# An encoder layer on one core: the first stage written in a new order, and silu(c) spread through a row in DRAM

## The chip, the cores and the metric

The kernel runs on one core of a Trainium2 chip. The core has five engines that run side by side, each through its own list of instructions, strictly in order: TensorE (PE in the profile, with its weight loads as PEld), VectorE (DVE), ScalarE (ACT), GpSimd (POOL) and SyncE (SP), which here issues the transfers (DMAs) between the device's memory and the on-chip memory. Engines wait for each other by semaphores. The metric is the device time of one execution in microseconds.

## The reference

One layer of an encoder over 2048 tokens of width 1024, batch 1, everything in float32. What matters for this change is how it begins:

```python
c_act = jax.nn.silu(c)                                   # c: 1024 numbers
mod = c_act @ ada_w[l] + ada_b[l]                        # 3 x 1024 numbers
shift, scale, gate = jnp.split(mod, 3, axis=-1)
h = (_layernorm(x) * (1.0 + scale[:, None, :]) + shift[:, None, :])
proj = h @ w_in[l]                                       # 1024 x 9216
...                                                      # recurrence and neighbourhood attention on proj's parts
y = jnp.concatenate([y_hg, y_na], axis=-1) @ w_out[l]
z = DEEPNORM_ALPHA * x + gate[:, None, :] * y
x = _layernorm(z) * ln_g[l] + ln_b[l]
```

## The kernel before

The first half of the tokens (1024) is held as two groups of 512 tokens, and the model's width as eight blocks of 128, called k = 0 to 7. A **piece** (g, k) is the part of h for group g and block k, turned so that the width lies on the partitions: 128 x 512 numbers, stored as a high and a low part (`h` tiles) because a product in float32 is made of three matmuls: high by high, low by high, high by low.

`startup` is the stage that the change touches. It makes all 16 pieces and multiplies each, as soon as it is there, with the weights of three projections (query, key and gate of the first attention pair), adding up over k in six PSUM tiles `acc`. Its parts, with the names and lines that the trace shows:

- **silu(c)**: `mod_init` loads c into all 128 partitions (`cb`, L133); `mod_silu` makes exp on ACT (L138), a cap on DVE (L318), Ln and Exp on ACT (L319, L320); the product is made in `startup` on DVE (L1197), between the second and the third tile of the norms.
- **modulation sums**: for each k, `mod_sum` (L150) makes two sums over 1024 products on DVE, one for `shift` and one for `scale`, from two 512 KB tiles `ada` of ada_w that `mod_load` (L145) fetches. Six such tiles fit, so a load waits for an earlier sum.
- **norms**: `x_stats` (L200, L201) takes mean and variance of the four tiles of 128 tokens of a group on DVE, `rstd_of` (L176 to L183) and L207 turn them into a factor and an offset by small steps on DVE and ACT, and `x_scale` (L214) applies them on ACT, to half of the width (four blocks) at a time.
- **a piece** (`h_piece`): four transposes on PE into PSUM (L221), scale and shift on ACT (L223, tile `sg`), the high part on ACT (L225), the low part on DVE (L228).
- **weights**: `w_load` (L1176) and `w_split`: high part on ACT (L1184), low part on DVE (L1185). They come in two halves, for k below 4 and from 4 on.
- **products**: `proj_mm` (L260), nine matmuls of 128x512 for each piece.

Within this stage the order of PE, SP, ACT and DVE is the order of the code. The list `order` says in which order the pieces are multiplied: group 0's first three, then group 1's first two, then alternating. `piece(g, k)` writes everything that the piece needs at the place of the piece: for group 0 its own modulation sum first, then transposes, scaling and split; for (1, 0) the whole norms of group 1 first. One piece ahead is written before the nine matmuls of the current one. So on PE the transposes of the next piece stand before the matmuls of the current piece.

After the stage, `first_half` begins: the six sums are copied out of PSUM (`evac`, L748), split into the tiles of the attention (q at L927 and L928, the copies `KA` and `KB` at L943, the gate at L958, L319, L320), while PE runs `vproj` (L273), a projection whose weights come in four tiles that are split at L800 and L801. The first two splits are made within `startup`, the third and fourth after the evacuations. In this part the order of PE is still that of the code; ACT, DVE and SP are ordered by a scheduler at build time. The results of vproj go out to DRAM (`nv`, L281) and come back in another layout (`V`, L952), which the attention's last product (L1074) reads. `gate_load` (L158, L161) fetches the rest of ada_w for the gate's sums, which use silu(c) from a DRAM row `c_d`.

Of the kernel before, what the change touches and what calls it, by code (L numbers as in the profile page):

```python
# [10 lines left out]
F32 = mybir.dt.float32  # L11
F32R = mybir.dt.float32r
U32 = mybir.dt.uint32
AF = mybir.ActivationFunctionType
ALU = mybir.AluOpType
# [22 lines left out]
def body(ctx: ExitStack, tc: tile.TileContext, t):  # L38
# [49 lines left out]
    def nm(s):  # L88
        cnt[0] += 1
        return f"{s}_{cnt[0]}"  # L90
# [40 lines left out]
    def mod_init():  # L131
        mod["c"] = tl("cb", shape=[P, D])
        dma(mod["c"], t["c"].rearrange("p k -> (p k)").rearrange("(o n) -> o n", o=1).to_broadcast([P, D]))  # L133

    def mod_silu():
        dve.tensor_scalar(adab1, adab[:, 8:16], 1.0, 1.0, op0=ALU.mult, op1=ALU.add)
        r = tl("nb", shape=[P, 3072])[:, 0:D]
        act.activation(r, mod["c"], AF.Exp, scale=-1.0)  # L138
        sigmoid(r)
        return r  # L140
# [54 lines left out]
    def x_stats(xs, pin=lambda x: x, between=None):  # L195
        mv = cp.tile([P, 4, 2], F32, tag="xmv", name=nm("xmv"), bufs=2)
        for i, xt in enumerate(xs):
            st = cp.tile([P, 2, 6], F32, tag="bnst", name=nm("bnst"), bufs=4)
            for a in range(2):
                pin(dve.bn_stats(st[:, a, :], xt[a]))  # L200
            dve.bn_aggr(mv[:, i, :], st)  # L201
            if i == 1 and between:
                between()
# [14 lines left out]
    def h_piece(xs, k, hi, lo, early=False):  # L218
# [5 lines left out]
        if early:  # L224
            act.activation(hi, tmp, AF.Copy)  # L225
        else:
            dve.tensor_copy(hi, tmp)
# [939 lines left out]
    def startup():  # L1167
# [25 lines left out]
        xs[1] = x_load(1)  # L1193
        for i in range(3):
            w_load(i, 1)
        r = mod_silu()
        how[0] = x_stats(xs[0], between=lambda: dve.tensor_mul(mod["c"], mod["c"], r))  # L1197
# [3 lines left out]
        order = [(0, 0), (0, 1), (0, 2), (1, 0), (1, 1), (0, 3), (1, 2), (0, 4), (1, 3), (0, 5), (1, 4), (0, 6), (1, 5), (0, 7), (1, 6), (1, 7)]  # L1201

        def piece(g, k):
            if g == 0:
                mod_sum(k)
                if k and k + 2 < KT:
                    mod_load(k + 2)
                if k == 0:
                    w_split(0, 0)
            elif k == 0:  # L1210
                how[1] = x_stats(xs[1])
                x_scale(xs[1], how[1], 0, 4)
            h_piece(xs[g], k, hts[g, k, 0], hts[g, k, 1], True)
            if (g, k) == (0, 0):
                w_split(1, 0)
                w_split(2, 0)
            elif (g, k) == (1, 1):
                x_scale(xs[0], how[0], 1, 4)
            elif (g, k) == (0, 3):
                for i in range(3):  # L1220
                    w_split(i, 1)
            elif (g, k) == (0, 4):
                x_scale(xs[1], how[1], 1, 4)

        piece(0, 0)
        for n, (g, k) in enumerate(order):
            if n + 1 < len(order):
                piece(*order[n + 1])
            if (g, k) == (0, 6):
                feed = Chunks(first_srcs())  # L1230
                rp = bias_rows()
                bias_fill()
                dma(lg, t["lb_logits"])
                dma(normg, t["hg_norm_g"])
            if (g, k) == (0, 7):
                bias_tables(rp)
                bias_pair(0)
                dma(c_d.rearrange("(o n) -> o n", o=1), mod["c"][0:1, :])
            if (g, k) in ((0, 7), (1, 6)):
                feed.split()  # L1240
            for i in range(3):
                proj_mm(acc[i, g], *ws[i], g, k)
            if (g, k) == (1, 7):
                for gg in range(2):
                    for i in range(3):
                        rows[NCOL[i][0]][gg] = evac(acc[i, gg])
# [353 lines left out]
```

## Time and profile before

| | us |
|---|---|
| three timed runs | 2669.26, 2673.63, 2672.89 |
| their median | 2672.89 |
| the execution that was profiled | 2663.61 |
| its span, from the first to the last instruction | 2661.8 |
| first matmul of the stage | 21.26 |
| first matmul of vproj, where the stage ends on PE | 89.45 |

The prediction quotes rows of views of one profiled execution. A row of a timeline has the start in us from the span's start, the duration, the engine, the line of the kernel, the operation, output<-input by the program's names, shapes and a count, and in brackets how long the engine sat idle before it and what released it. A row of waits has the engine and line that waited, what it waited for, the total, the number of times and the longest. A row of windows has the busy time of each engine in a stretch, the granted clock of TensorE and the share of the DMA engines. The chain is the work that ended last, followed backwards; within it "DMA a<-b" is the time until that transfer landed. "SPq" rows are SP issuing a transfer.

### The profile page before, as it was taken

What the parts mean: (1) busy time and instruction counts of PE and PEld (TensorE: products, weight loads), DVE (VectorE), ACT (ScalarE), POOL (GpSimd) and SP (SyncE); (2) the same over time, 40 slices, a digit from 0 to 9 for tenths busy, and PEclk for the clock granted to TensorE, in tenths of its full rate; (3) what the DMA queues carried; (4) which work ended last, traced back from release to release, by engine and by line L of the source; (5) the groups of instructions that cost most, each with busy time, mean ns of one, the idle gap of its engine ahead of it and who ended that gap; (6) DMA issues with size and microseconds to landing.
All of it is one profiled execution on the core that took longest, in us unless ns stands there. A gap on an engine that the chain in (4) does not pass through costs nothing.

```text
span 2661.8 us, 46149 instructions
## 1 busy us (share of the span) xinstructions
PE 2574.7 (97%) x17328; PEld 2151.1 (81%) x17328; DVE 1761.2 (66%) x4351; ACT 1417.6 (53%) x2808; POOL 105.3 (4%) x143
## 2 busy tenths in 40 slices
PE   4999999999999999999999999999999997999998
PEld 3888888888888888888888888887888886788887
DVE  5445445477777778877777877456877886548443
ACT  4434444376666667666666665355666665331110
POOL 0000000000000000000000000000000000032221
PEclk8999999999999999999999999999999998999999
DMA  6555454212222227312221122354444456554331
GB/s 232 169 176 161 144 179 139 99 64 100 84 80 80 88 96 252 105 58 76 72 80 60 65 72 79 101 165 114 124 135 139 130 144 168 143 158 131 95 95 56
DMA packets 235777, 313.25 MB, mean 118 GB/s; under 512 B 29480, under 2 KB 118312, under 8 KB 235433
## 3 DMA queue, kind: packets, MB, share of 16 engines
q1 hardware_dynamic: 235553, 310.30, 37.8%
q8 instruction: 136, 2.23, 0.4%
q14 instruction: 88, 0.72, 0.1%
HBM read 226.63 MB, written 75.37 MB: 113 GB/s over the span
## 4 chain that ended last, share of the span: by engine, by line
PE 87%; DVE 5%; DMA 4%; ACT 3%; issue 1%; SPq 0%; DVEq 0%; ACTq 0%
PE pj L260 49%; PE pj L273 5%; PE ps L1431 4%; PE ps L1430 4%; PE ps L1432 4%; PE ps L1074 3%; PE ps L1055 3%; PE ps L473 2%; PE ps L1006 2%; PE ps L465 1%; PE ps L1010 1%; PE ps L540 1%; PE ps L564 1%; PE ps L566 1%; PE ps L512 1%; DMA V<-nv 1%
## 5 line engine op out<-in xcount | busy, mean ns | idle before, releaser
L260 PE MATMUL pj<-h,wh 128*128 128x512 f32 x4016 | 1278.0, 399 | 10.6 <-ACT h L225 6.3
L260 PEld LDWEIGHTS pj<-h,wh 128*128 128x128 f32 x4016 | 730.9, 188 | 168.7 <-issue 13.1
L260 PE MATMUL pj<-h,wl 128*128 128x512 f32 x2008 | 785.8, 391 | 0.1
L260 PEld LDWEIGHTS pj<-h,wl 128*128 128x128 f32 x2008 | 377.2, 188 | 82.0 <-DVE wl L775 0.5
L1028 ACT ACTIVATE pbuf<-pbuf,mx 128x480 f32<-128x480 f32 (+2 forms) x224 | 143.1, 640 | 159.4 <-DVE mx L1023 158.5
L1023 DVE CUSTOM_DVE_ANT_1 pbuf<-ps,bias 128x480 f32<-128x480 f32 (+2 forms) x224 | 125.5, 589 | 117.5 <-PE ps L1010 95.7
L273 PE MATMUL pj<-wh,h 128*128 128x256 f32 x1024 | 193.6, 287 | 2.8 <-ACT vt L279 2.5
L273 PEld LDWEIGHTS pj<-wh,h 128*128 128x128 f32 x1024 | 162.7, 193 | 6.1 <-ACT vt L279 3.4
L251 DVE TENSOR_TENSOR wl<-wr,wh 128x512 fp32r<-128x512 f32 x192 | 131.5, 685 | 45.7 <-ACT wh L250 44.4
L250 ACT ACTIVATE wh<-wr 128x512 fp32r<-128x512 f32 x192 | 120.0, 625 | 73.2 <-PE pj L260 62.6
L273 PE MATMUL pj<-wl,h 128*128 128x256 f32 x512 | 145.5, 284 | 0.3 <-DVE wl L801 0.3
L1059 DVE COPY pt<-ps 128x512 f32<-128x512 f32 (+1 forms) x128 | 79.0, 618 | 58.9 <-PE ps L1055 58.1
L1061 ACT ACTIVATE pt<-ps 128x512 f32<-128x512 f32 (+1 forms) x128 | 68.9, 539 | 91.1 <-PE ps L1055 89.9
L459 DVE TENSOR_TENSOR de<-e,de 128x512 f32<-128x512 f32 x64 | 44.3, 692 | 109.2 <-ACT de L458 108.7
L748 ACT ACTIVATE e<-pj 128x512 f32<-128x512 f32 x100 | 59.1, 592 | 96.6 <-PE pj L260 85.7
L1055 PE MATMUL ps<-ident,pbuf 128*128 128x128 f32 x776 | 103.8, 274 | 1.5 <-DVE pt L1059 1.5
L1055 PEld LDWEIGHTS ps<-ident,pbuf 128*128 128x128 f32 x776 | 91.2, 141 | 15.5 <-DVE pt L1059 1.7
L1406 ACT ACTIVATE yh<-yr 128x512 fp32r<-128x512 f32 x52 | 32.7, 628 | 132.8 <-PE ps L1431 114.4
L1479 DVE TENSOR_TENSOR vt<-ps,gt 128x512 f32<-128x512 f32 x24 | 16.5, 691 | 127.1 <-PE ps L1432 127.1
L273 PEld LDWEIGHTS pj<-wl,h 128*128 128x128 f32 x512 | 98.8, 193 | 1.3 <-DVE wl L801 0.5
L1033 DVE TENSOR_SCALAR pbuf<-pbuf,mx 128x480 f32<-128x480 f32 (+2 forms) x224 | 95.7, 436 | 5.5
L801 DVE TENSOR_TENSOR wl<-wr,wh 128x512 fp32r<-128x512 f32 x68 | 46.8, 690 | 78.7 <-ACT wh L800 68.2
(273 smaller groups left out, 4757.3 us busy)
## 6 DMA issues: line engine op xcount, KB each, us to landing
wr<-in_w_in SPq DMA_DIRECT2D x276, 256.0 KB
V<-nv SPq DMA_DIRECT2D x256, 64.0 KB
yr<-yq SPq DMA_DIRECT2D x60, 256.0 KB
bias<-tint SPq DMA_DIRECT2D x24, 480.0 KB
x<-in_x SPq DMA_DIRECT2D x32, 256.0 KB
ada<-in_ada_w SPq DMA_DIRECT2D x16, 512.0 KB
wr<-in_w_v SPq DMA_DIRECT2D x32, 256.0 KB
nv<-vt SPq DMA_DIRECT2D x32, 256.0 KB
```

Of the source, the lines that this page charges most:

```text
L250: act.activation(hi, raw, AF.Copy)
L251: dve.tensor_tensor(lo, raw, hi, op=ALU.subtract)
L260: pe.matmul(pz, a, b, start=(k == 0 and n == 0), stop=(k == KT - 1 and n == 2))
L273: pe.matmul(pzs[tp][:, i * 256:(i + 1) * 256], a, b, start=(k == 0 and n == 0 and i == 0), stop=(k == KT - 1 and n == 2), skip_group_check ...
L1023: return dve.tensor_tensor_reduce(s[:, 0:nk].rearrange("p (r c) -> p r c", c=32), sc[:, 0:nk].rearrange("p (r c) -> p r c", c=32), bt[:, 0 ...
L1028: act.activation(s[:, 0:nk], s[:, 0:nk], AF.Exp, scale=-1.0, bias=mx[:, 0:1], accum_out=mx[:, 1:2])
L1033: dve.tensor_scalar(s[:, 0:nk], s[:, 0:nk], mx[:, 2:3], 1.0, op0=ALU.mult, op1=ALU.mult)
L1055: pe.transpose(ptp[:, c * P:(c + 1) * P], s[:, c * P:(c + 1) * P], ident)
L1074: pe.matmul(self.po[R][hs_, j * P:(j + 1) * P], self.st.V[c0 + c][:, j * P + hh * 64:j * P + hh * 64 + 64], pts[hh][:, c * P:(c + 1) * P], ...
L1430: pe.matmul(pz, yh[:, kk], wh, start=first, stop=False)
L1431: pe.matmul(pz, yh[:, kk], wl, start=False, stop=False)
L1432: pe.matmul(pz, yl[:, kk], wh, start=False, stop=last)
```

## The change

It rewrites the first stage. Nothing else of the program is edited; line numbers after it are a few higher.

- silu(c) is made on a 128 x 8 tile `cs` and not on 128 copies of c. The 4 KB result is written to the DRAM row `c_d` and read back from there into all partitions (`cb`). Both transfers are issued by ACT; no other transfer of the program is. The store of `c_d` that SP made at the end of the stage is gone.
- `x_stats` is split in `x_stat` (one tile) and `x_rate`, so that the norms of group 1 can be written tile by tile.
- `h_piece` gives its last step, the low part on DVE, back as a function, so that other work can be written between the high and the low part.
- Two tables, `ahead` and `after`, say what is written with which piece: the modulation sum of k stands with an earlier piece, the norms of group 1 with pieces (0, 2) and (0, 3), the splits of the second half of the weights with (1, 0), `x_scale` for the second half of the width with (1, 1).
- The order of the pieces has four of group 0 first.
- As a result of the scheduler's work, not of the text: in `first_half` SP now issues eight loads for the gate's sums (L161) ahead of the first loads V; before, all of them stood behind the first of those.
- On SP the loads of the sums of k = 3 come before the second group's x, and later loads are asked for one sum earlier.

```diff
     def mod_init():
         mod["c"] = tl("cb", shape=[P, D])
-        dma(mod["c"], t["c"]....to_broadcast([P, D]))
...
+        cs = [cp.tile([P, KT], F32, name=f"cs{i}") for i in range(2)]
+        dma(cs[0], t["c"])
+        act.activation(cs[1], cs[0], AF.Exp, scale=-1.0)
+        sigmoid(cs[1])
+        dve.tensor_mul(cs[1], cs[0], cs[1])
+        act.dma_start(c_d.rearrange("(p k) -> p k", k=KT), cs[1])
+        act.dma_start(mod["c"], c_d.rearrange("(o n) -> o n", o=1).to_broadcast([P, D]))
...
         if early:
             act.activation(hi, tmp, AF.Copy)
-        else:
-            dve.tensor_copy(hi, tmp)
+            return lambda: dve.tensor_tensor(lo, tmp, hi, op=ALU.subtract)
...
-        order = [(0, 0), (0, 1), (0, 2), (1, 0), (1, 1), (0, 3), (1, 2), (0, 4), (1, 3), ...
+        def mod_step(k):
+            mod_sum(k)
+            if k + 3 < KT:
+                mod_load(k + 3)
...
+        order = [(0, 0), (0, 1), (0, 2), (0, 3), (1, 0), (1, 1), (0, 4), (1, 2), (1, 3), ...
+        ahead = {(0, 0): [(mod_step, 1)], (0, 1): [(mod_step, 2)], (0, 2): [(mod_step, 3), (second_stats, 0)], (0, 3): [(second_stats, 1, 2, 3)],
...
         def piece(g, k):
-            if g == 0:
-                mod_sum(k)
...
+            low = head(g, k)
+            for f, *a in ahead.get((g, k), []):
+                f(*a)
+            low()
```

**ACT, at the start of the program.** `cb` is silu(c) or c in all partitions, `nb` a scratch tile, `cs` the small tile, L178 the first of ACT's two steps of group 0's norms. Before:

```order
L107 ACT_TABLE_LOAD
L138 ACTIVATE nb_194<-cb_136 128x1024
L319 ACTIVATE nb_194<-nb_194 128x1024
L320 ACTIVATE nb_194<-nb_194 128x1024
L178 ACTIVATE l_220<-v_218 128x4
```

And now:

```order
L107 ACT_TABLE_LOAD
L135 ACTIVATE cs_138<-cs_137 128x8
L323 ACTIVATE cs_138<-cs_138 128x8
L324 ACTIVATE cs_138<-cs_138 128x8
L138 DMA c_d<-cs_138 128x8
L139 DMA cb_136<-c_d 128x1024
L178 ACTIVATE l_204<-v_202 128x4
```

The three wide operations became three narrow ones, and two transfers stand ahead of L178; the second waits for the first to land.

**DVE, in the first pieces.** `h_96` and `h_98` are low parts of pieces (0, 1) and (0, 2); the pairs of L150 with two `ada` tiles are the sums of one k. Before, from the low part of (0, 1) on, where the sums belong to k = 2 and the statistics are those of group 1:

```order
L228 TENSOR_TENSOR h_96<-sg_273,h_95 128x512
L150 ISA ada_170,shift<-ada_170,cb_136,adab 128x1024
L150 ISA shift 128x1
L150 ISA ada_172,scale_86<-ada_172,cb_136,adab_84 128x1024
L150 ISA scale_86 128x1
L228 TENSOR_TENSOR h_98<-sg_297,h_97 128x512
L200 BN_STATS bnst_311<-x_174 128x6
L200 BN_STATS bnst_311<-x_175 128x6
```

And now, from the sums of k = 2 on, which are followed by those of k = 3:

```order
L150 ISA ada_180,shift<-ada_180,cb_136,adab 128x1024
L150 ISA shift 128x1
L150 ISA ada_182,scale_86<-ada_182,cb_136,adab_84 128x1024
L150 ISA scale_86 128x1
L230 TENSOR_TENSOR h_96<-sg_281,h_95 128x512
L150 ISA ada_226,shift<-ada_226,cb_136,adab 128x1024
L150 ISA shift 128x1
L150 ISA ada_228,scale_86<-ada_228,cb_136,adab_84 128x1024
L150 ISA scale_86 128x1
L204 BN_STATS bnst_314<-x_230 128x6
L204 BN_STATS bnst_314<-x_231 128x6
L205 BN_AGGR xmv_223<-bnst_314 128x2
```

The sums of a k stand one low part earlier, those of k = 3 were moved ahead of the statistics of group 1, and the low part `h_98` (not in these rows) now follows the first tile's statistics.

**ACT, at the end of the stage.** `e` are the six sums copied out of PSUM, `KA`, `KB` the key tiles, `sg` the gate, `wh` the third and fourth weight tile of vproj. Before:

```order
L748 ACTIVATE e_674<-ps_236 128x512
L958 ACTIVATE sg_724<-e_672 128x512
L748 ACTIVATE e_676<-ps_237 128x512
L748 ACTIVATE e_678<-ps_238 128x512
L319 ACTIVATE sg_724<-sg_724 128x512
L320 ACTIVATE sg_724<-sg_724 128x512
L800 ACTIVATE wh_731<-wr_558 128x512
L800 ACTIVATE wh_737<-wr_560 128x512
L943 ACTIVATE KA_163_697<-e_670 64x512
L943 ACTIVATE KB_164_698<-e_670 64x512
```

And now:

```order
L752 ACTIVATE e_676<-ps_220 128x512
L947 ACTIVATE KA_162_699<-e_672 64x512
L947 ACTIVATE KB_163_700<-e_672 64x512
L962 ACTIVATE sg_726<-e_674 128x512
L752 ACTIVATE e_678<-ps_221 128x512
L752 ACTIVATE e_680<-ps_222 128x512
L947 ACTIVATE KA_162_699<-e_678 64x256
L947 ACTIVATE KB_163_700<-e_678 64x256
L323 ACTIVATE sg_726<-sg_726 128x512
L324 ACTIVATE sg_726<-sg_726 128x512
L804 ACTIVATE wh_733<-wr_507 128x512
L804 ACTIVATE wh_739<-wr_509 128x512
```

The four key copies, which stood behind the two weight splits, now stand ahead of them; DVE's low parts moved in the same way.

More of the change, by code (lines that the diff above doesn't have):

```diff
@@ L193, in x_load, with x_stats, x_stat, x_rate @@
         return xs
-    def x_stats(xs, pin=lambda x: x, between=None):
+    def x_stats(xs, pin=lambda x: x):
         mv = cp.tile([P, 4, 2], F32, tag="xmv", name=nm("xmv"), bufs=2)
[L197 to L203, printed above, removed]
+        for i in range(4):
+            x_stat(xs[i], mv[:, i, :], pin)
+        return x_rate(mv)
+    def x_stat(xt, mv, pin=lambda x: x):
+        st = cp.tile([P, 2, 6], F32, tag="bnst", name=nm("bnst"), bufs=4)
+        for a in range(2):
+            pin(dve.bn_stats(st[:, a, :], xt[a]))
+        dve.bn_aggr(mv, st)
+    def x_rate(mv):
         r = cp.tile([P, 4], F32, tag="xr", name=nm("xr"), bufs=2)
@@ L1192, in startup @@
         mod_load(2)
[L1193 to L1197, printed above, removed]
+        how[0] = x_stats(xs[0])
         x_scale(xs[0], how[0], 0, 4)
@@ L1200, in startup @@
         rows = {n: [None, None] for n, _ in NCOL}
-        order = [(0, 0), (0, 1), (0, 2), (1, 0), (1, 1), (0, 3), (1, 2), (0, 4), (1, 3), (0, 5), (1, 4), (0, 6), (1, 5), (0, 7), (1, 6), (1, 7)]
-        def piece(g, k):
-            if g == 0:
-                mod_sum(k)
[L1206 to L1223, printed above, removed]
+        mv1 = cp.tile([P, 4, 2], F32, tag="xmv", name=nm("xmv"), bufs=2)
@@ new lines, in startup, with second_x, second_stats, head @@
+        more = {}
+        def mod_step(k):
+            mod_sum(k)
+            if k + 3 < KT:
+                mod_load(k + 3)
+        def second_x():
+            xs[1] = x_load(1)
+            for i in range(3):
+                w_load(i, 1)
+        def second_stats(*tiles):
+            for i in tiles:
+                x_stat(xs[1][i], mv1[:, i, :])
+            if 3 in tiles:
+                how[1] = x_rate(mv1)
+                x_scale(xs[1], how[1], 0, 4)
+        def head(g, k):
+            return h_piece(xs[g], k, hts[g, k, 0], hts[g, k, 1], True)
@@ L1225, in startup @@
+        def piece(g, k):
+            low = head(g, k)
+            for f, *a in ahead.get((g, k), []):
+                f(*a)
+            low()
+        mod_step(0)
+        second_x()
+        w_split(0, 0)
         piece(0, 0)
+        w_split(1, 0)
+        w_split(2, 0)
         for n, (g, k) in enumerate(order):
@@ L1228, in startup @@
                 piece(*order[n + 1])
[L1229 to L1240, printed above, removed]
+            for f, *a in after.get((g, k), []):
+                f(*a)
             for i in range(3):
                 proj_mm(acc[i, g], *ws[i], g, k)
[L1243 to L1246, printed above, removed]
+        for gg in range(2):
+            for i in range(3):
+                rows[NCOL[i][0]][gg] = evac(acc[i, gg])
+        feed = more["feed"]
         return rows, feed
```

23 lines of the change are left out of this document (17 added, 6 removed).

## Prediction

> **What bounds the kernel now.** The page first: PE is the bound of the whole.
>
> ```profile
> span 2661.8 us, 46149 instructions
> PE 2574.7 (97%) x17328; PEld 2151.1 (81%) x17328; DVE 1761.2 (66%) x4351; ACT 1417.6 (53%) x2808; POOL 105.3 (4%) x143
> ```
>
> PE lacks 87.1 us of the span. So the question is where PE idles, and I cut the first stage into windows at its breaks.
>
> ```profile
> core 0: us, PE busy (x) PEld busy (x) DVE busy (x) ACT busy (x) POOL busy (x), PEclk, DMA share, GB/s
> 0.00:17.20 17.20, 0.00 (x0) 0.00 (x0) 9.44 (x22) 5.79 (x8) 3.99 (x11) 1.00 0.89 316
> 17.20:29.90 12.70, 10.16 (x30) 6.43 (x30) 9.24 (x16) 6.38 (x10) 0.00 (x0) 1.00 1.04 396
> 29.90:43.20 13.30, 1.93 (x6) 0.98 (x6) 7.46 (x21) 4.74 (x8) 0.00 (x0) 0.59 0.40 161
> 43.20:89.40 46.20, 39.20 (x175) 29.25 (x174) 25.52 (x44) 28.15 (x44) 1.07 (x5) 0.97 0.39 116
> ```
>
> PE is idle 17.2, 2.5, 11.4 and 7.0 us, 38.1 of the 87.1. These are three different waits, and the view of waits up to 125 us and PE's timeline say which:
>
> ```profile
> PE ps L221 <- ACT x L214: 29.2, 8, 17.2
> ACT sg L223 <- DVE scale L150: 20.2, 7, 3.5
> PE pj L260 <- ACT h L225: 6.3, 7, 1.4
> ...
> 40.65 0.47 PE L221 MATMUL ps<-ident,x 128*128 128x128 f32 x1 [10.68 <-ACT x L214]
> 42.89 1.20 PE L260 MATMUL pj<-h,wh 128*128 128x512 f32 x2
> 46.48 0.60 PE L221 MATMUL ps<-ident,x 128*128 128x128 f32 x4
> 49.00 0.60 PE L221 MATMUL ps<-ident,x 128*128 128x128 f32 x4
> 89.45 0.28 PE L273 MATMUL pj<-wh,h 128*128 128x256 f32 x1
> ```
>
> The wait on L214 is for normalized tokens, once at the start (17.2) and once for group 1 (10.68). The second row is the repeated one: ACT waits 20.2 us for modulation sums, 2.9 each, and PE then for ACT. A piece that waits for nothing takes 49.00 - 46.48 = 2.52 us on PE. DVE's timeline shows why both waits are long:
>
> ```profile
> 7.11 0.69 DVE L318 TENSOR_SCALAR nb<-nb 128x1024 f32<-128x1024 f32 x1 [4.43 <-ACT nb L138]
> 7.72 1.28 DVE L200 BATCH_NORM_STATS2 bnst<-x 128x6 f32<-128x512 f32 x2
> 10.55 1.19 DVE L1197 TENSOR_TENSOR cb<-cb,nb 128x1024 f32<-128x1024 f32 x1
> 16.07 0.16 DVE L207 SCALAR_TENSOR_TENSOR xb<-xmv,xr 128x4 f32<-128x4 f32 x1
> 16.15 1.28 DVE L150 CUSTOM_DVE_ANT_0 ada<-ada,cb,adab 128x1024 f32<-128x1024 f32 x1
> 18.57 0.08 DVE L150 DVE_READ_ACCUMULATOR2_ANT scale<- 128x1 f32 x1
> 32.38 1.28 DVE L200 BATCH_NORM_STATS2 bnst<-x 128x6 f32<-128x512 f32 x2
> 39.58 0.16 DVE L207 SCALAR_TENSOR_TENSOR xb<-xmv,xr 128x4 f32<-128x4 f32 x1
> ```
>
> A pair of sums takes 2.42 us (16.15 to 18.57), two tiles of statistics 2.83 (7.72 to 10.55), all of group 1's norms 7.4 (32.38 to 39.74), during which nothing else is written. Afterwards DVE is busy only 25.5 of 46.2 us: each sum comes just too late, with free time between.
>
> **The change part by part.** First, silu(c). The chain's first rows:
>
> ```profile
> 1.20 4.80 DMA cb<-in_c
> 6.02 4.52 DMA x<-in_x
> ...
> 0.75 0.39 SPq L121 DMA_DIRECT2D adab<-in_ada_b  x1
> 2.52 0.17 DVE L136 TENSOR_SCALAR adab<-adab 128x8 f32<-128x8 f32 x1 [2.52 <-DMA adab<-in_ada_b]
> ...
> 96.16 0.47 SPq L1238 DMA_DIRECT2D c_d<-cb  x1
> 98.61 0.45 POOL L722 MEMSET bias<- 64x192 f32 x2 [12.46 <-DMA c_d<-cb]
> ```
>
> The load of c took 4.8 us, and x's last tile was issued only when it had landed (6.02): 512 KB that go. A small load landed 1.77 us after its issue, the 4 KB store 2.45. DVE loses the cap of 0.69 and the product of 1.19 in front of and inside the statistics. Without both, statistics begin with x's first tile, which I put at 4.4 (issue 1.7, latency 1.77 as adab, 0.65 for 256 KB at the 400 GB/s of the second window, rounded up); four tiles take 5.7, the small steps 1.7 (10.55 + 1.19 and two more tiles make 14.57, L207 ends at 16.23): ready at 11.8, say 12.0, in place of 16.2.
>
> On ACT: c lands at 3.0 (1.2 + 1.77), three narrow operations and two on DVE end at 4.3 (0.26 each, of which L207 shows 0.16 and the rest is handing over), the store lands at 6.8, and until then ACT stands still. Behind it is queued L178, which is due at 10.5, so the wait costs nothing, with 3.7 us to spare. The spread then takes 4.8 us as the load of c did: landed at 11.6, when the first sums are due at 12.0. This is the unknown: no transfer of this trace is issued by ACT. The nearest rows bound it from below at 9.9 (1.77 plus 1.3 for the bytes, behind nothing) and from above at 18, if it stands behind what SP has issued (worked out under the rivals). From 13 on (ACT's `x_scale` and the transposes, until 15.5, cover about 1 us) each us late costs one.
>
> [...]
>
> Then DVE is one chain up to group 1's norms, and I add it up: sums of k = 0 from 12.0 to 14.4; the first weight split waits for its high part on ACT behind four `x_scale` (2.93 below) until 15.5 and ends at 16.1; sums of k = 1 to 18.6; three 0.6 us subtractions to 20.4; sums of k = 2 to 22.8; one subtraction, sums of k = 3 to 25.9; a tile's statistics to 27.3; a subtraction, three tiles to 32.2; small steps to 34.0. So group 1's norms are ready at 34.0, not 39.7, with one k more of sums done. The loads keep up: up to those of k = 3 it is 7.6 MB, at 400 GB/s from 2.2 on until 21.2, and I allow 24.6 for latency and the spread; group 1's x lands by 30. The pieces (0, 0) to (0, 2) go by beside it.
>
> ```profile
> 39.78 2.93 ACT L214 ACTIVATE x<-x,xb,xr 128x512 f32<-128x512 f32 x4 [1.02 <-DVE xb L207]
> ```
>
> On PE the transposes of (1, 0) still stand ahead of the matmuls of the piece before it, now (0, 3). So these start 3.1 us after the norms, as before (39.78 to 42.89): at 37.1, a gain of 5.8. Behind that point before had 14 pieces and took 46.6 us (42.89 to 89.45). Now it has 13: 32.8 us at 2.52; 1.5 for the slow clock of the first (42.89 to 46.48, where nine matmuls at full clock take 2.1); 2.1 for (0, 4), whose transposes wait for the second `x_scale`, written only with (1, 1); some 1.5 in small waits at (1, 0), (1, 2) and (0, 6). The sums cost nothing now, as each stands at least one low part ahead and DVE has room (13 low parts and four pairs of sums are 17.5 of 38 us). Together 37.9: the stage ends at 75.0, not 89.45, a gain of 14.4.
>
> At (0, 4) PE idles 2.1 us. In this trace idles up to 1.4 us left the clock up, 10.68 brought it down (window three, 0.59). If 2.1 did, nine matmuls would cost 1.5 more; it is nearer to 1.4, so I take none. [...]
>
> Last, what follows the stage. The key copies stand ahead of vproj's third and fourth weight tile now:
>
> ```profile
> 93.19 1.14 ACT L800 ACTIVATE wh<-wr 128x512 fp32r<-128x512 f32 x2
> 94.24 0.61 ACT L943 ACTIVATE KA<-e 64x512 fp32r<-64x512 f32 x1
> 95.97 0.42 ACT L943 ACTIVATE KB<-e 64x256 fp32r<-64x256 f32 x1
> 93.93 1.29 DVE L801 TENSOR_TENSOR wl<-wr,wh 128x512 fp32r<-128x512 f32 x2
> 89.62 23.26 PE pj L273 x192
> ```
>
> vproj takes 0.121 us a matmul, and needs its third tile after 48, 5.8 us after its start (95.2). Before, the tile's low part was done at 94.6. The four copies take 2.15 us (94.24 to 96.39) and some 0.2 in order; the tile is then ready 7.5 us after the start, so PE waits 1.7. Bounds: 0, if the copies hide in ACT's waits, and 2.4. I take 1.7, since ACT's rows follow each other without a wait (the splits of 93.19 are through at 94.24).
>
> SP's gate loads, now ahead of the V loads, touch this place:
>
> ```profile
> 123.27 1.02 SPq L281 DMA_DIRECT2D nv<-vt  x2
> 130.34 2.77 SPq L952 DMA_DIRECT2D V<-nv  x5
> 133.75 1.28 PE L1074 MATMUL ps<-pt,V 128*64 128x128 f32 x16 [0.47 <-DMA V<-nv]
> ```
>
> The third V tile was the tight one. Its store waited on SP until 123.27 behind other loads, which now stand earlier; I take no change, between a gain of 0.5 and a loss of 4 (six 256 KB loads at 0.65 us).
>
> Sum: 14.4 - 1.7 = 12.7 us. The profiled execution took 2663.61 us, with 1.8 around its span, and would take 2650.9. The three runs' median is 9.3 us above it; the sum is taken off the median: 2672.89 - 12.7 = 2660.2.
>
> **The rivals.** *ACT's transfers queue behind SP's.* For: SP always has several out. At 4.4 some seven loads of x are, so the store would land near 8; the spread would stand behind eight transfers of x, `ada` and weights, 2.6 MB or 6.5 us, and with 3.3 for its own bytes (4.8 less 1.5 of latency) land at 18. The stage ends 5.0 later, at 80.0: gain 7.7, 2665.2. Against: nothing in the trace.
>
> *ACT's transfers are served only when SP's are all through*, the one that ends slower. SP's list stops by itself, since the second sums' buffers must come free first: the store would go at about 12, after x and the first `ada`, and land at 14, the spread after the next 2.6 MB at 22, landing at 26.5. DVE's chain then starts 14.5 us later, the stage ends at 88.5, and with vproj's 1.7 the kernel is 0.8 us slower: 2673.7. The point from which it decides is a landing after 25.7; for more than 0.2% (5.3 us) slower, after 31. Against: it needs strict priority on both trips.
>
> *V comes late*: the gate loads take the engines from the stores and the third tile lands 4 us late. Gain 8.7: 2664.2. For: the row at 133.75 has no slack. Against: its store has fewer issues ahead.
>
> *The gain is given back*: the stage ends early, but some later transfer sets a time of its own. 2669 to 2673. Against: after 89.45 PE's rows have one wait of 0.47 up to 150 us.
>
> **How the numbers follow.** The forecast has 0.68, the queue behind SP 0.13, late V 0.09, strict priority 0.06 (half of it beyond 0.2%), the gain given back 0.04. A measurement of this kernel can tell about 0.2% from no change; three of the cases are past it on the fast side: faster 0.9, same 0.07 (the last case and half of strict priority), slower 0.03. The low end is the gain without vproj's wait and V's (14.9: 2658.0), less 2 for the runs' scatter of 4.4: 2656. The high end is the first rival with 1.5 for the clock (2666.7), plus 2: 2669.
>
> **What would show it.** Right: group 1's L207 near 34, PE's first transposes of group 1 near 35, vproj's first matmul near 75 and one wait of 1 to 2 us in it on DVE's `wl`; ACT no longer waits for `scale` after 40 us. Wrong: the first L150 later than 13 with `cb` as its releaser (the transfer), a clock below full after 46 us, L1074 waiting for V by several us, or vproj starting near 89.

## The result: faster by more than forecast, and a large part of it not from the stage

| | before | after |
|---|---|---|
| timed runs, median (us) | 2673.26 (2669.26 to 2677.19, 4 runs) | 2650.98 (2648.58 to 2656.49, 4 runs) |
| ratio, 95% interval | | 0.9925 (0.9913 to 0.9936) |
| profiled execution, its span | 2663.61, 2661.8 | 2650.65, 2648.4 |
| first matmul of vproj | 89.45 | 79.90 |

The forecast was 2660.2 with a range down to 2656. The kernel became about 20 us faster by the ratio, 13.0 by the two profiled executions. The stage itself gave 9.55 us (89.45 to 79.90) of the 14.4 foretold, and at 147 us 7.1 are left of the 12.7 foretold. So two things need a cause: the stage gave less than foretold, and something behind it gave some 13 us more.

The page of after, its first lines:

```profile
span 2648.4 us, 46154 instructions
PE 2575.1 (97%) x17328; PEld 2152.4 (81%) x17328; DVE 1761.3 (67%) x4351; ACT 1415.2 (53%) x2808; POOL 105.4 (4%) x143
```

PE is busy as long as before (2574.7); the 13.4 us of the span are idle time. The stage in the same windows as before:

```profile
0.00:17.20 17.20, 1.18 (x3) 0.55 (x3) 8.01 (x21) 4.85 (x10) 3.93 (x11) 1.00 0.77 251
17.20:29.90 12.70, 8.19 (x24) 5.94 (x24) 12.02 (x20) 5.92 (x10) 0.00 (x0) 1.00 1.03 402
29.90:43.20 13.30, 7.00 (x27) 4.68 (x26) 8.39 (x22) 6.14 (x11) 0.23 (x1) 0.87 0.82 319
43.20:89.40 46.20, 42.92 (x225) 34.78 (x224) 27.99 (x48) 32.91 (x53) 1.23 (x6) 0.96 0.52 151
```

The long idle time in front of group 1 (third window, PE 1.93 before) is partly filled, and the sums no longer hold PE up behind it. The timeline of after, several engines:

```profile
5.23 0.34 ACTq L138 DMA_DIRECT2D c_d<-cs  x1
9.24 0.69 DVE L204 BATCH_NORM_STATS2 bnst<-x 128x6 f32<-128x512 f32 x1 [1.98 <-DMA x<-in_x]
12.43 0.33 ACTq L139 DMA_DIRECT2D cb<-c_d  x1
14.47 0.16 DVE L211 SCALAR_TENSOR_TENSOR xb<-xmv,xr 128x4 f32<-128x4 f32 x1
17.88 1.28 DVE L150 CUSTOM_DVE_ANT_0 ada<-ada,cb,adab 128x1024 f32<-128x1024 f32 x1 [3.24 <-DMA cb<-c_d]
38.35 0.16 DVE L211 SCALAR_TENSOR_TENSOR xb<-xmv,xr 128x4 f32<-128x4 f32 x1
41.65 1.20 PE L264 MATMUL pj<-h,wh 128*128 128x512 f32 x2
79.90 0.28 PE L277 MATMUL pj<-wh,h 128*128 128x256 f32 x1
```

The first L150 is released by `cb` and starts at 17.88, 5.9 us later than forecast; from there on everything keeps the forecast's distances. The store took 7.2 us from its issue to that of the spread, which waits for it (5.23 to 12.43), the spread 5.45 (12.43 to 17.88). After the stage, in the waits of PE up to 150 us:

```profile
PE ps L1078 <- DMA V<-nv: 1.3, 2, 0.9
PE pj L277 <- ACT wh L804: 0.7, 1, 0.7
PE pj L277 <- DVE wl L805: 0.4, 1, 0.4
```

The third weight tile costs 1.1 us (1.7 forecast), V 0.8 more than before. In the two profiles of after and two others with its stage (lane_after and pad2_after, below) the matmul that lies at 146.88 in before comes 7.7 us earlier on average than in the eight profiles with before's stage (139.8 against 147.4). That is what the stage gives for good.

The rest shows up late. Matmul against matmul, after is 7.1 us ahead of before at 1650 us, 4.3 at 1850, 3.9 at 2200 and 13.4 from 2390 to the end; in the second pair of profiles (again_before and again_after, below) it is 8.6, 13.1, 13.6 and 17.1. From 1650 to 1850 us, where a few of SP's rows stand in another order, the two pairs disagree: one loses 2.8 us and the other gains 4.5. What both gain (9.5 and 3.5) is at the start of the last attention pair, from 2230 us on, where all engines' rows stand as before. The waits of PE from 2190 to 2300 us, before, then after:

```profile
PE ps L1006 <- issue: 13.6, 1, 13.6
PE pj L1430 <- DMA wo<-wod: 4.6, 1, 4.6
```

```profile
PE ps L1010 <- issue: 10.6, 1, 10.6
PE pj L1452 <- DMA wo<-wod: 0.5, 1, 0.5
```

What stands behind the 13.6 us is in the timeline of before:

```profile
2231.77 0.60 SPq L718 DMA_DIRECT2D bias<-tint  x1
...
2242.43 0.56 DVE L1023 CUSTOM_DVE_ANT_1 pbuf<-ps,bias 128x384 f32<-128x384 f32 x1 [5.09 <-DMA wo<-wod]
...
2247.75 0.52 SPq L944 DMA_DIRECT2D KA<-KA  x1
...
2253.44 0.74 PE L1006 MATMUL ps<-KA,Q 128*128 128x480 f32 x1 [13.59 <-issue]
```

A bias tile, issued at 2231.77 behind weights, is waited for by DVE until 2242.43 (5.09 us idle). The row names `wo`, the weights around it; that it is the bias tile follows from what the row reads, and in a kernel further below (pad3_before) the same row names the tile:

```profile
2236.52 0.56 DVE L1025 CUSTOM_DVE_ANT_1 pbuf<-ps,bias 128x384 f32<-128x384 f32 x1 [0.92 <-DMA bias<-tint]
```

The next scores follow only after that and after the key tile's copy has gone through a transfer. PE's clock falls in the idle time (0.88 granted from 2200 to 2300 us). The place waits for transfers (DVE starts 10.7 us after the bias tile's issue, PE 5.7 us after the key copy's at 2247.75), and its length differs between executions too (12.9 and 3.2 us in again_before, below).

### The profile page after: what moved, and what is told of

Its sections match the earlier page's. It is cut to its first block, busy times and chain, and to the rows that moved or that the text cites. A ratio compares the mean times of both kernels' runs of the same rounds, so it can differ in the third digit from the quotient of the medians.

```text
span 2648.4 us, 46154 instructions
## 1 busy us (share of the span) xinstructions
PE 2575.1 (97%) x17328; PEld 2152.4 (81%) x17328; DVE 1761.3 (67%) x4351; ACT 1415.2 (53%) x2808; POOL 105.4 (4%) x143
## 4 chain that ended last, share of the span: by engine, by line
PE 88%; DVE 4%; DMA 4%; ACT 3%; issue 1%; SPq 0%; DVEq 0%; ACTq 0%
PE pj L264 49%; PE pj L277 5%; PE ps L1453 4%; PE ps L1451 4%; PE ps L1452 4%; PE ps L1078 3%; PE ps L1059 3%; PE ps L477 2%; PE ps L1010 2%; PE ps L469 1%; PE ps L544 1%; PE ps L1014 1%; PE ps L568 1%; PE ps L570 1%; PE ps L516 1%
## 5 line engine op out<-in xcount | busy, mean ns | idle before, releaser
L264 PEld LDWEIGHTS pj<-h,wh 128*128 128x128 f32 x4016 | 731.1, 188 | 164.1 <-issue 13.1
L805 DVE TENSOR_TENSOR wl<-wr,wh 128x512 fp32r<-128x512 f32 x68 | 46.8, 690 | 80.8 <-ACT wh L804 75.7
```

The lines of the kernel that those rows point to most:

```text
L264: pe.matmul(pz, a, b, start=(k == 0 and n == 0), stop=(k == KT - 1 and n == 2))
```

## The experiments

Each was timed in five rounds beside the kernel before. Ratios are to before, with the 95% interval.

| kernel | ratio | interval | vproj starts (us) |
|---|---|---|---|
| again_before | 1.0001 | 0.9991 to 1.0011 | 91.91 |
| again_after | 0.9941 | 0.9924 to 0.9958 | 81.15 |
| order_only | 0.9956 | 0.9939 to 0.9972 | 79.56 |
| row_only | 0.9986 | 0.9973 to 0.9998 | 90.81 |
| pe_spread | 0.9906 | 0.9892 to 0.9919 | 77.20 |
| store_first | 0.9941 | 0.9928 to 0.9955 | 82.34 |
| sums_own | 0.9942 | 0.9931 to 0.9954 | 83.22 |
| lane_before | 0.9971 | 0.9959 to 0.9984 | 89.76 |
| lane8_before | 0.9997 | 0.9987 to 1.0008 | 89.21 |
| memset_before | 0.9969 | 0.9958 to 0.9981 | 89.17 |
| lane_after | 0.9923 | 0.9910 to 0.9936 | 80.17 |
| lane_pe | 0.9902 | 0.9887 to 0.9917 | 75.87 |
| pad2_before | 0.9953 | 0.9940 to 0.9966 | 91.63 |
| pad2_after | 0.9933 | 0.9919 to 0.9947 | 79.57 |
| pad3_before | 0.9943 | 0.9930 to 0.9955 | 91.36 |
| pe_third_pad | 0.9940 | 0.9927 to 0.9953 | 77.14 |
| pad2_order | 0.9923 | 0.9907 to 0.9938 | 79.65 |
| pad7_before | 0.9921 | 0.9905 to 0.9937 | 89.99 |

### First question: which part brings it, and is the late place chance

Theory A took the extra for scatter of the late place; theory B for a steady effect of the new phase. The two kernels as they are, again:

> The kernel before, unchanged, beside itself. Ratio 1.000 within 0.2%. Theory A (the stage gave 7.7 us, and what the result shows beyond that, some 5 to 12 us, is scatter of a late place, the start of the last attention pair at 2230 to 2290 us, which differs between executions of one kernel): this second profile has another idle time there than the first one had (PE at L1006 13.6 us, at L1430 for wo 4.6, and 23.9 us at the half clock between 2240 and 2300), and its span differs from 2661.8 by 4 us or more. Theory B (the late place is slow in every execution of before, since transfers and scaling there fall into each other at this phase, and the new order shifts them): the same rows return, within 2 us.

Measured: 1.0001, 2670.82 us. The late place returned at 12.9 and 3.2 us for `wo` (13.6 and 4.6), but this execution took 10.0 us more span, 2.5 of them in the first stage and some 6 from 1700 to 1850 us. So single executions do differ, by as much as the sum in question, and neither theory is settled by one.

> The changed kernel, unchanged, against before. Ratio 0.9925 within 0.15% (20 us), as first measured, by both theories. Its second profile: first sums at 17.9 and vproj from about 79.9 again, as these are set by the list of instructions and the queue. Theory A: between 2230 and 2330 us it loses another amount than the first profile did (PE at L1010 10.6 us, 13.6 us at the half clock), and its gain on before lies elsewhere along the run than before. Theory B: the same amount within 2 us.

Measured: 0.9941, 2656.44 us; vproj at 81.15, since `cb` came at 19.11; the late place 11.1 us. A gain of 16 us by the ratio, with every one of the five runs (2652.64 to 2657.16) below all 23 of before (2664.10 at the lowest): scatter is not the cause of it.

```diff
 def mod_init():        # order_only: as before the change
+    dma(mod["c"], t["c"]....to_broadcast([P, D]))
-    act.dma_start(c_d..., cs[1])
-    act.dma_start(mod["c"], c_d...to_broadcast([P, D]))
```

> The changed kernel with the kernel before's silu(c): c loaded by SP into all partitions, wide operations, the product between two tiles of the norms, the row stored by SP late. If the row by way of ACT's queue costs what it looks like (first sums at 17.88, where before had them at 16.15), then without it the first sums start at about 16.2, the stage ends 1.7 us earlier (vproj from about 78.2), and the time is 1 to 2 us below that of the changed kernel: ratio to before about 0.992. Rival: the row is what brings the gain (statistics no longer have the cap, the product and the late x before them, so x is free earlier); then the stage ends later than 80 and at least half of the 20 us is gone: ratio 0.996 or more.

Measured: 0.9956, 2658.30 us. First sums 16.30 and vproj 79.56, only 0.34 earlier than in after, since x comes later behind the load of c; the time was 12 us below before by the ratio. Neither side of the expectation: the stage is as good as in after, yet 4 to 8 us of the gain are missing (8 against after; against again_after, timed beside it, the intervals overlap).

```diff
 def mod_init():        # row_only: the kernel before, with the small tile and the row
-    dma(mod["c"], t["c"]....to_broadcast([P, D]))
+    act.dma_start(c_d..., cs[1])
+    act.dma_start(mod["c"], c_d...to_broadcast([P, D]))
```

> The kernel before, in its old order, with the small silu(c) and the row in DRAM by ACT's queue. If the transfer's delay costs its full amount: first sums at 17.9 instead of 16.15, first matmul at about 23 instead of 21.3, and the rest of the stage as before, with group 1's norms 0 to 2 us later: 0 to 2 us slower, ratio 1.000 to 1.001. Rival (the row brings the gain): faster by 5 us or more, ratio 0.998 or less.

Measured: 0.9986, 2666.93 us: 4 us faster, though its first sums start at 18.65 (16.15 in before) and the matmul that lies at 146.88 in before comes at 150.39, later than in all eight profiles with before's stage (146.5 to 149.5). The row costs early on, as foretold, and yet the kernel isn't slower. Not all of that cost is the row's: the scheduler put the key copies ahead of vproj's weight tiles here too, and PE waits the 1.1 us for the third tile as in after. So the kernels with the row had something of their own that the stage doesn't show.

### Second question: what held the spread up

```diff
-        act.dma_start(c_d.rearrange("(p k) -> p k", k=KT), cs[1])
+        dma(c_d.rearrange("(p k) -> p k", k=KT), cs[1])      # SP, ahead of x
```

> The changed kernel, with the store of the row issued by SP right behind the load of c and ahead of all loads of x, so that nothing is in front of it; the spread stays with ACT. It asks what the store's 7.2 us are. Theory queue (it stood behind x): the store takes 2 to 3 us, the spread is issued at about 8 and lands at 13 to 14. Theory fixed (32-byte pieces from 128 partitions, or ACT's queue, take that long by themselves): the store takes 6 us or more and the spread lands at 17 or later. In both, x comes 3.5 us later, the norms are there at about 18 instead of 14.6, and the stage ends within 1.5 us of that of the changed kernel; ratio to before 0.993 to 0.995.

The timeline of store_first:

```profile
5.23 0.33 SPq L138 DMA_DIRECT2D c_d<-cs  x1
6.68 0.34 ACTq L139 DMA_DIRECT2D cb<-c_d  x1
13.75 1.48 DVE L204 BATCH_NORM_STATS2 bnst<-x 128x6 f32<-128x512 f32 x2 [3.54 <-DMA x<-in_x]
20.16 1.28 DVE L150 CUSTOM_DVE_ANT_0 ada<-ada,cb,adab 128x1024 f32<-128x1024 f32 x1
```

The same store, from the same tile at the same moment, takes 1.45 us with nothing in front (5.23 to 6.68) and took 7.2 behind the loads of x. The spread's last packet ended at 13.36. The queue theory holds; 32-byte pieces are not the cost. (The store goes by SP's queue here, which is a second difference. But the spread, still on ACT's queue, started its packets 1.8 us after its issue, with x issued on SP's from 5.61 on: ACT's queue alone doesn't account for the 7.2.) x paid for it (norms at 20.2), so the kernel is no faster: 0.9941.

```diff
+        for j in range(2):
+            pt = ps("hx")
+            for k in range(4):
+                pe.transpose(pt[:, k * P:(k + 1) * P], cs[1][:, 4 * j + k:...].to_broadcast([P, P]), ident)
+            act.activation(cv[:, 4 * j:4 * j + 4, :], pt..., AF.Copy)
```

> The changed kernel, but silu(c) is spread by TensorE and not by way of DRAM: eight transposes of a column of the 128 x 8 tile, repeated 128 times, into two PSUM tiles, which ACT copies out into cb; the row c_d is stored by SP late, as before. No transfer is issued by ACT. If the step that failed is the landing of the spread (17.9 and 19.1 in the two profiles, 11.6 forecast), the first sums start at 13.6 to 15, right behind the norms of group 0, group 1's norms are there at about 34.5 to 36, the stage ends 3 to 5 us earlier than in the changed kernel (vproj from 75 to 77), and the time is 2 to 5 us lower: ratio to before 0.992 to 0.9925. Rival: the weights' and ada's transfers do not keep up, so that DVE waits for ada instead; then less than 1.5 us is gained.

The timeline of pe_spread:

```profile
6.47 2.00 ACT L143 ACTIVATE cb<-ps 128x512 f32<-128x512 f32 x2 [1.47 <-PE ps L142]
14.01 1.28 DVE L154 CUSTOM_DVE_ANT_0 ada<-ada,cb,adab 128x1024 f32<-128x1024 f32 x1
35.68 0.16 DVE L215 SCALAR_TENSOR_TENSOR xb<-xmv,xr 128x4 f32<-128x4 f32 x1
77.20 0.28 PE L281 MATMUL pj<-wh,h 128*128 128x256 f32 x1
```

`cb` is complete at 8.47, the sums start right behind the norms at 14.01, group 1's norms come at 35.68 and vproj at 77.20, 2.7 us earlier than in after. 0.9906, 2646.98 us. The sums and the norms came as expected, vproj 0.2 us behind the 75 to 77 named, and the time below the range named (0.992 to 0.9925). The transfers keep up: DVE has no wait for `ada` here.

```diff
-        ahead = {..., (1, 1): [(mod_step, 4), ...], (1, 2): [(mod_step, 5)], (0, 5): [(mod_step, 6)], (0, 6): [(mod_step, 7)]}
+        ahead = {..., (1, 1): [...]}
+            if g == 0 and k >= 4:
+                mod_step(k)
             low = head(g, k)
```

> The changed kernel, with the modulation sums of k = 4 to 7 written ahead of their own piece, as before the change, and not one or two pieces ahead; the piece order and the rest stay. If the early sums bring the second part of the stage's gain (38.2 us from the matmuls of (0, 3) to vproj, where 14 pieces took 46.6), ACT waits 2 to 3 us for scale at each of the four again, PE 0.9 to 2.9 each, and the stage ends 3.6 to 10 us later: ratio to before 0.9955 to 0.998. Rival (the new piece order brings it): the stage ends less than 1.5 us later and the ratio stays at 0.9945 or below.

Measured: from the matmuls of (0, 3) at 41.45 to vproj at 83.22 it takes 41.8 us, 38.25 in after, 46.56 in before. Of the 8.3 us that this part of the stage gave, 2.5 are a piece that now lies ahead of it (14 before, 13 now, 2.52 each), the early sums of k = 4 to 7 bring about 3.5, and some 2.3 are left for the piece order. The stage ends 3.3 us later than in after, just under the 3.6 to 10 named. Of these, vproj's stretch gives 1.7 back (V is not waited for here), and the time is 0.9942, as in again_after: expected was 0.9955 or more, which failed.

### Third question: what the other half of the gain is

In the trace of before the 1,510 transfers, all SP's, use eight semaphores in turn, and from the ninth on (4.54 us) the wait for the one eight before stands in the row or just ahead of it in 1,338 of 1,502. The row adds one transfer and turns the later ones by one: so it is with all 1,190 of the last 1,200 that can be matched between before and after.

```diff
                 dma(normg, t["hg_norm_g"])
+                dma(cp.tile([P, 1], F32, name="spare"), t["hg_norm_g"])
```

> The kernel before with one transfer more, of 512 bytes into a tile that nothing reads, late in the first stage; no other row of any engine moves. Each of SP's transfers waits for that of eight before, and the extra one turns by one which of the eight semaphores each later transfer uses, as the row in DRAM did. In the three profiles with the row, PE's stretch from 2100 to 1700 instructions before the end took 70.0 to 64.7, 60.4 and 64.1 us less than without it: with the row 64.7, 60.4, 64.1 as differences of start, without it 70.0, 67.7, 73.0, less 15.3 for the last hundred in each. If that turn is the cause: 60 to 65 here too, and 4 us faster than before, ratio 0.9985. If it is chance between executions: anything from 60 to 73, and ratio 1.000 within 0.1%.

(The stretch meant runs from the 2100th to the 1800th matmul before the end: 70.0, 67.7 and 73.0 us without the row, 64.7, 60.4 and 64.1 with it.) Measured: 66.8 us there, and 0.9971: a transfer of 512 bytes that nobody waits for makes the kernel before 7.8 us faster, twice what was expected. It looked like the turn. Two tests of that:

> The kernel before with eight of the 512-byte transfers in the place where one made it 7.8 us faster (0.9971, 0.9959 to 0.9984). Eight turn the eight semaphores of SP's transfers once round, so that every later transfer has the one that it had before. Theory turn (which semaphore a transfer uses sets the time of the late places): the gain is gone, ratio 1.000 within 0.15%. Theory place (one transfer more at this place shifts SP against the other engines): a gain of 5 us or more stays, ratio 0.998 or less, as eight issues of 0.4 us shift SP more than one.

> The kernel before with a memset of 512 bytes on GpSimd in that place, into a tile that nothing reads; no transfer and no other row moves. It asks whether any edit, however small, ends the state of before. Theory turn and theory place: nothing changes, ratio 1.000 within 0.1%. Theory of chance between builds (each build of the program has late places of its own): anything between 0.996 and 1.002.

For the first, the loop makes eight of the tile and its transfer; for the second the line is this:

```diff
-                dma(cp.tile([P, 1], F32, name="spare"), t["hg_norm_g"])
+                pool.memset(cp.tile([P, 1], F32, name="spare"), 0.0)
```

Eight transfers: 0.9997, as the turn has it. But a memset on GpSimd, with no transfer and no semaphore turned: 0.9969, as much as the transfer. The theory of the turn falls, and that of the place with it.

The single transfer in the changed kernel, and in the one that spreads by TensorE:

> The changed kernel with one of these transfers more at the corresponding place. The row in DRAM has already turned the semaphores by one against before, this turns them by one again. Theory turn: a change of 3 us or more either way against the changed kernel, not foretold which (the second position has not been measured). Theory place: 0 to 8 us faster, as before was. If the state of before was the odd one and all others are alike: within 2 us of the changed kernel, ratio 0.993 to 0.9945.

> The kernel that spreads silu(c) by TensorE (ratio 0.9906, on the semaphores of before) with one of these transfers more. Theory turn: 5 to 8 us faster than without, about 2640, ratio 0.988. Theory place: the same. If only the very state of before is slow: within 2 us of 2647, ratio 0.990 to 0.9913.

Measured: 0.9923 and 0.9902, against 0.9925 and 0.9941 for after, and 0.9906 for pe_spread: no difference that can be measured. So the state of before is the odd one. What all these edits share is a small tile: each takes 32 bytes in every partition, and all tiles allocated after it move up. In the built programs most of the large tiles, V, KA and `yr` among them, begin modulo 256 bytes at 32 in before, order_only and lane8_before (8 x 32 is a whole turn), at 64 in lane_before and memset_before, at 96 in after and the others with the two tiles `cs`, at 128 in lane_after and lane_pe, which have three. Moving the addresses alone, with no instruction added or moved:

```diff
     adab = cp.tile([P, 24], F32, name="adab")
+    for i in range(2):        # pad2; 3 in pad3, 7 in pad7
+        cp.tile([P, 1], F32, name=f"spare{i}")
```

> The kernel before with two spare tiles of 4 bytes a partition that nothing writes or reads: no instruction is added or moved, every later tile lies 64 bytes higher, at 96 beyond a multiple of 128 as in the changed kernel. Theory address (transfers into tiles at 32 beyond a multiple of 128 are the slowest, and the late places hang on transfers): 8 to 10 us faster, ratio 0.9960 to 0.9972, and of the 73,728 packets of 512 bytes some 13,000 take over 28 ns instead of 24,000. The changed kernel is then only 7 to 10 us faster than this one, which is what its stage gave. Rival (the small tile's instructions, or chance between builds): ratio 1.000.

> The kernel before with three spare tiles: the tiles lie on multiples of 128. Theory address: at least as fast as with two, 9 to 13 us faster than before, ratio 0.995 to 0.9965, and under 5,000 packets of 512 bytes above 28 ns. Rival: 1.000, or a state of its own.

> The kernel before with seven spare tiles without an instruction: all later tiles on multiples of 256. At 32, 64, 96 and 128 before took 2670, 2663, 2657 and 2654, and 21,300, 17,100, 10,600 and 4,800 of the 512-byte packets took over 28 ns; at 160 the changed kernel had 11,750. If both follow the distance from 128 within 256 bytes, this one is no faster than before, ratio 0.999 to 1.002, with 21,000 packets or more. If multiples of 128 are all alike: ratio 0.994, under 5,000 packets.

| large tiles at, modulo 256 | kernels with before's stage | ratio | 512-byte packets over 28 ns, of 73,728 | matmuls 2100 to 1800 before the end (us) |
|---|---|---|---|---|
| 32 | before, again_before, lane8_before | 1, 1.0001, 0.9997 | 21,299, 21,472, 21,665 | 70.0, 67.7, 70.8 |
| 64 | lane_before, memset_before | 0.9971, 0.9969 | 17,080, 17,073 | 66.8, 65.0 |
| 96 | pad2_before | 0.9953 | 10,603 | 65.2 |
| 128 | pad3_before | 0.9943 | 4,798 | 62.4 |
| 0 | pad7_before | 0.9921 | 2,825 | 58.0 |

With no instruction changed (the rows of all five engines are the same, in the same order, in before, pad2_before and pad7_before), the addresses alone are worth up to 0.8%, as much as the whole change (0.9921 against 0.9925). From 64 on, neighbours in the table overlap in their intervals; 32 is apart from all others. Matmul against matmul, pad7_before gains 11.9 us on before and 9.7 on again_before between 2200 and 2390 us; from 1650 to 1850 it loses 3.8 on the one and gains 4.4 on the other. So the steady part lies at the start of the last pair. That the slow packets are the way from the address to the time is argued from the table, not shown: row_only has 11,215 of them, nearly as few as pad2_before, and gained 0.14% to its 0.47%; its early cost, 2 to 3 us, is a third of that difference. The 28 ns is a bound chosen for counting; the mean of all 73,728 is 30.1 ns in before and 27.8 in pad7_before. The waits of PE from 2190 to 2300 us in pad3_before and pad7_before, beside the 13.6 and 4.6 of before:

```profile
PE ps L1008 <- issue: 8.9, 1, 8.9
PE pj L1432 <- ACT yh L1424: 1.8, 1, 1.8
PE pj L1432 <- DMA wo<-wod: 1.3, 1, 1.3
```

```profile
PE ps L1008 <- issue: 6.5, 1, 6.5
PE pj L1432 <- ACT yh L1424: 1.7, 1, 1.7
PE pj L1432 <- DMA wo<-wod: 1.1, 1, 1.1
```

The bias tile there is issued at 2230.58 and DVE starts on it at 2239.99 without having waited. The kernels with two and three spare tiles gained somewhat more than expected. For 0 I had the choice between as slow as 32 and 0.994; it is 0.9921, the fastest, and has the fewest slow packets (2,825). No run shows by what way the address sets the time of a packet, and why 32 is the worst (21,299) stays open.

> The changed kernel with two such spare tiles: all later tiles 64 bytes higher, at 160, which is 32 beyond a multiple of 128, as the kernel before has them. Theory address: 7 to 10 us slower than the changed kernel, at about 2663, ratio to before 0.9965 to 0.9975, with the stage unchanged (vproj from 79 to 81). Rival: as the changed kernel, 0.9925 to 0.994.

Measured: 0.9933, no slower. At 160 it has 11,751 slow packets, as after at 96 (10,514), so a period of 128 bytes, on which that expectation stood, is wrong. No kernel with the new order and the row was run at 32; order_only is the nearest, and there the new order brings 0.9956.

Last, order_only with two spare tiles:

> The new order with the kernel before's silu(c) (as order_only), and two spare tiles without an instruction, so that all later tiles lie at 96 as in the changed kernel. By the address: 8 to 13 us faster than order_only, 2646 to 2651, ratio 0.9912 to 0.993. If the row costs what its late landing says (1 to 3 us), this is 1 to 3 us faster than the changed kernel's 2651 to 2656. If the row brings something of its own, it is slower than 2655.

Measured: 0.9923, 2649.65 us, 8.7 below order_only, with vproj at the same moment (79.65): what order_only lacked was the address. In the two profiles, 19.5 us apart, pad2_order is ahead by 1.2 us at 1640, 6.1 at 2200 and 19.5 from 2390 on. At 96 the four combinations are now complete:

| at 96 | old order | new order |
|---|---|---|
| c spread by SP | 0.9953 (pad2_before) | 0.9923 (pad2_order) |
| row in DRAM | 0.9986 (row_only) | 0.9925, 0.9941 (after, again_after) |

At equal addresses the new order brings 8 us, the row costs: 0.5 to 5 us in the new order (within the intervals of nothing), 9 in the old, of which the profiles show at most 3.5 in the stage and vproj; where the rest goes is open. The whole change brings 3 to 7.5 us at equal addresses (7.7 by the profiles up to 147 us); its two small tiles bring 12.6, 0.0047 of 2671. The split depends on where one starts: by way of order_only the order brings 11.8 us and the addresses 8.8. The intervals, some 3.5 us to each side, leave room for both.

### A version put together

```diff
-  ... (1, 6): [(lambda: more["feed"].split(),)]}
+  ... (1, 6): [(lambda: more["feed"].split(),)], (1, 7): [(lambda: more["feed"].split(),)]}
```

> The version put together: silu(c) spread by TensorE, one spare tile without an instruction (tiles on multiples of 128), and the third weight tile of vproj split one step earlier, with the last piece of the stage, so that it does not stand behind the key copies. The later stream of weight splits starts one tile earlier by that. Expected: about 2642 as the kernel with the spread and one transfer (2642.6), less the 1.1 us that PE waited for the third tile: ratio 0.987 to 0.9905. Rival: the earlier stream takes buffers or transfers from others later on, and it is 2 us or more slower than 2642.

Measured: 0.9940, some 10 us slower than lane_pe; the rival held. The waits of PE from 70 to 400 us:

```profile
PE pj L282 <- ACT vt L288: 4.1, 1, 4.1
PE ps L1064 <- DVE mx L1041: 2.4, 1, 2.4
PE ps L1064 <- DVE pbuf L1042: 1.3, 1, 1.3
```

The stream of splits runs one tile earlier, the scheduler orders ACT and DVE anew behind it, and new waits cost several times the 1.1 us won: at 392 us lane_pe, which has none of these three waits, is 11.5 us ahead. The fastest measured is lane_pe, the spread by TensorE with tiles at 128: 2642.61 us, 0.9902, against 0.9925 and 0.9941 for the changed kernel; from pe_spread (0.9906, at 96) it can't be told apart.

## Why the prediction was wrong, point by point

- **The step that failed first: "The spread then takes 4.8 us as the load of c did: landed at 11.6".** It landed at 17.88, as the first rival had it (18), and the stage ended at 79.90 where that rival said 80.0. The spread's own duration was near (5.45); the term that was mis-sized is the store in front of it, priced at 2.45 from a row issued with little in flight (DMA share 0.22 from 94 to 96 us), which took 7.2 behind x (share 0.96 from 5.2 to 12.4). store_first shows why (1.45 with nothing ahead), pe_spread what it cost: 2.7 us at the end of the stage. I had given this rival 0.13. That it hit the 18 is partly luck: it had the store land near 8 and the spread take 10 behind eight transfers, where 12.43 and 5.45 were measured; two errors cancel. (The 1.5 us of latency in it is an estimate: `adab` landed 1.77 us after the start of its issue, 1.38 after its end.)
- **The rest of that step.** Even with `cb` ready early (pe_spread) the sums start at 14.01, not 12.0: the first statistics began at 5.19 and not 4.4, DVE waited 1.98 us for x, and the cap on the 128 x 8 tile took 1.21 us where 0.26 was taken, which made the store a microsecond late. The timeline of after has a neighbour for this cap, a memset on GpSimd that in before came at 11.80, behind the product on DVE, and that the change set free to run at the start:

```profile
1.83 2.66 POOL L689 MEMSET nb<- 128x3072 f32 x1
3.31 1.21 DVE L322 TENSOR_SCALAR cs<-cs 128x8 f32<-128x8 f32 x1 [3.31 <-ACT cs L135]
```

The memset ends at 4.49 and the cap at 4.52. The prediction had no term for it.
- **The chain behind it was right.** From the first sums to group 1's norms 22.0 us were added up; after took 20.6 (17.88 to 38.51), pe_spread 21.8. The matmuls of (0, 3) start 3.1 us behind the norms, as foretold, and from there 37.9 were forecast, 38.25 measured. ACT waited for `scale` twice, 2.9 us, the last time at 23.49; the second `x_scale` held the transposes of (0, 4) up four times, 0.16 to 0.38 us, and PE's clock stayed up behind them (1.00 granted from 48 us on; 0.52 from 40 to 46.8, behind the 4.62 us that PE idled before group 1's transposes). That the 2.1 us foretold there would have left it up was not safe: before's own trace has half the clock from 1759.5 to 1762.9, right behind an idle time of 2.50 us (1757.92), and full clock behind one of 2.94 (1808.55).
- **vproj**: 1.1 for 1.7; V 0.8 within its bounds. The stretch behind the stage, up to 147 us, lengthened by 2.5 in all; 0.6 of it is in neither.
- **The term that was missing, and the larger error.** The sum took for granted that nothing changes behind vproj, since "nothing else of the program is edited". But `cs` is two new tiles, and 64 bytes more in front of every large tile bring 12.6 us by themselves (pad2_before). Neither the four rivals nor the range had a place for that: the range ended at 2656, and stage and addresses come to 2652.6 (2672.89 less 7.7 and 12.6). So of the gain some 7 to 8 us are the stage, near the first rival's 7.7, and some 9 to 13 the addresses. Why the address changes the time of the late places stays open.

## What to carry to other kernels

Here every added tile, one of 4 bytes in a partition too, moved the addresses of the later tiles by 32, and seven of them were worth 0.8% of the time (pad7_before, 0.9921): run the old kernel with the same shift before the gain is put down to the change, and try a few shifts for their own sake. A transfer issued by ACT was not free of what SP had in flight (the 4 KB store took 7.2 us in after, 1.45 with nothing ahead); price it by what is queued at that moment, or keep a small vector on the chip, as the eight transposes did (vproj at 77.20 in place of 79.90).

## What the runs showed of the hardware

- The start address of tiles, modulo 256 bytes, changed how many 512-byte packets are slow (2,825 to 21,665 of 73,728 above 28 ns) and, with no instruction changed, the time by 19 us of 2671. The busy time of DVE and ACT does not move with it (1761.2 and 1417.6 us in before, 1761.8 and 1417.8 in pad7_before).
- A 4 KB store took 1.45 us with nothing ahead of it (store_first), and 5.7 to 7.2 us in six profiles with loads of x in flight on the other queue. The two queues are apart in the trace of after (q1 has SP's packets, q10 the 288 of ACT's two transfers); the store's packets, issued at 5.23 there, started from 8.17 to 11.83 us.
- The cap on 128 x 8 numbers ended at 4.51 to 4.52 us in all ten profiles that have it, whether it began at 3.31 or at 4.06, and GpSimd's memset of `nb` at 4.49 to 4.50; on 128 x 1024, at 7.11 in before with no memset beside it, it took 0.69. So in these profiles the cap went on until the memset was through. The statistics on DVE that met the same memset in before (11.80 to 14.46) took their usual 0.64 to 0.69. No run moved the memset alone.
